# The last expert's six held weight loads are issued in order, and the running sum is loaded from GpSimd's queue and used behind the branch

## The chip, the cores and the metric

The kernel runs on one core of one Trainium2 chip. The metric is device time in microseconds of one launch; the time before is the median of three runs. A profile is one further execution, taken by the hardware profiler. Times inside it are counted from the span's start. The engines are named as in the profile: PE (TensorE matmuls), PEld (its weight loads), DVE (VectorE), ACT (ScalarE), POOL (GpSimd), SP (SyncE, which here only issues transfers).

## The reference, cut to what matters

One layer of a decoder: a token mixer, a layer norm, a mixture of 32 experts of which each token takes four, and a second layer norm. The change touches only the end of the mixture.

```python
def moe_ffn(x2, w_router, b_router, w_gu, b_gu, w_down, b_down):
    ...                                     # top 4 of 32 experts per token, softmax gates
    def expert_block(args):
        tok, e = args
        xb = x_pad[tok]
        h = xb @ w_gu[e] + b_gu[e]          # 1024 -> 2048
        gate = jnp.minimum(h[:, 0::2], SWIGLU_LIMIT)
        up = jnp.clip(h[:, 1::2], -SWIGLU_LIMIT, SWIGLU_LIMIT)
        act = (up + 1.0) * (gate * jax.nn.sigmoid(SWIGLU_ALPHA * gate))
        return act @ w_down[e] + b_down[e]  # 1024 -> 1024
    ...
    out = jax.ops.segment_sum(y, slot_tok, num_segments=t_tok + 1)[:t_tok]

x = layer_norm(DEEPNORM_ALPHA * x + m, ln2_g[l], ln2_b[l])   # m is moe_ffn's output
```

There are 512 tokens of width 1024, all in float32.

## The kernel before, in words

The experts run one after another. Expert e has twelve weight tiles of 1 MB each: eight gu tiles (k = 0 to 7, rows of `w_gu`) and four dn tiles (rows of `w_down`, two k each). `wload` (L585) hands them out in this order over a ring of 19 buffers and issues each load on SP's queue. SP works through its queue strictly in order, and a load is issued only when the third load before it has landed (`PACE` = 3).

For one expert PE runs 24 units: sixteen gu units (in the last expert k by k, two halves `a` = 0 and 1 for each k), then eight dn units (units j = 16 to 23, k = 0 to 7). A unit is two matmuls in the program, which the trace counts as four. Between the units stand the steps of the activation: `act(e, a)` (L1053 to L1057 on DVE and ACT) makes 256 columns of the activation per half, `act_t(e, a)` transposes them on PE (L1030) and copies them to `at` on ACT (L1140). dn units k = 0 to 3 need `act_t(e, 0)`, those with k = 4 to 7 need `act_t(e, 1)`. Each expert's result is then added to `accd`, the running sum in HBM, by an indirect transfer from POOL's queue (L946, a scatter with add).

The last expert's result doesn't go through `accd`. Instead the running sum comes back on chip as two loads of 1 MB (`load_sum`, tiles FT in ring buffers named `gw`), which have to wait for expert 30's scatter. For each of the four blocks t of 128 tokens, `split_sum` makes a rounded high part on ACT (L1259) and the remainder on DVE (blocks 0 to 2) or POOL (block 3) (L1262). `last_sum` (L1264) then adds up in PSUM, per block and half q: gates times the down bias (L1270, from `b`, which needs `b_down`), and the two parts of the sum (L1272). `last_bias` (L1249) makes `b` out of the three small `b_down` loads (L1216): one cast on ACT (L1251) and one subtraction on POOL (L1252). After the last dn unit ACT and DVE make `ys` from the dn result, `last_y` adds it for each block (L1289), and the second layer norm and the stores follow.

Behind unit j = 17 stands a branch on all engines (`tc.If(cmax > 192)`, L1411) to a general path for experts with more than 192 tokens. It isn't taken with these inputs, but every engine has to pass it.

Of the last expert `wload` only allocates the last six tiles (`HELD` = 6: gu k = 6 and 7, and the four dn tiles) and keeps their loads back. `last_loads` (L1209), which runs behind unit 0 of the last expert, issues on SP first the two loads of the sum, then the three of `b_down`, then the six that were held. The splitting of the sum stands behind unit 11 (`BJ`), the sums of block 0 behind unit 15 (`SJ`), those of block 1 behind the branch, those of block 2 behind unit 19. The program's order is the order on each engine: there is no reordering.

Of the kernel before, what the change touches and what calls it, by code (L numbers as in the profile page):

```python
# [33 lines left out]
def hybrid_kernel(ctx, tc, x, w_in, b_in, conv_a, w_out_a, w_pool, scale_pool, conv_c, conv_c_b,  # L34
                  ln_c_g, ln_c_b, w_out_c, b_out_c, w_o, ln1_g, ln1_b, w_router, b_router,
                  w_gu, b_gu, w_down, b_down, ln2_g, ln2_b, out, dbg=None):
    nc = tc.nc
# [451 lines left out]
    for i, (kind, c, post) in enumerate(steps):  # L489
# [7 lines left out]
        if kind == "yb" and (c | 1) not in PLH:  # L497
            while fg:
                q, f, f2 = fg.popleft()
# [28 lines left out]
        while fg:  # L528
            q, f, f2 = fg.popleft()
# [42 lines left out]
    wjobs = []  # L572
# [6 lines left out]
    wn = [0]  # L579
    wpools = [(wB1, "wb1")] * 4 + [(wA, "w")] * 3 + [(wB2, "wb2")] * 2 + [(wA, "w")] + [(wB2, "wb2")] * 2  # L580
    RING = 12 + NB3 + 4

    lds, held = [], []

    def wload(n):  # L585
        for _ in range(n):
            if wn[0] >= len(wjobs):
                return
            key, src = wjobs[wn[0]]
            pool, tag = wpools[wn[0] % RING]  # L590
            shp = [128, 2 * D] if key[0] == "gu" else [128, 2, D]
            t_ = pool.tile(shp, F32, name="w", tag=tag)
            def ld(t_=t_, src=src):
                i = nc.sync.dma_start(t_, src).ins
                if len(lds) >= PACE:
                    tc.add_manual_dep(i, lds[-PACE].name, mybir.DependencyInfo(
                        mybir.DependencyClass.Sync, mybir.DependencyReason.DATA), reason="a few loads under way at a time")
                lds.append(i)
            held.append(ld) if wn[0] >= len(wjobs) - HELD else ld()
            W[key] = t_  # L600
            wn[0] += 1

# [230 lines left out]
    def split_wo(n):  # L833
        for a in range(2):
            wo_split(n, a, *((split, ("wh", "wl")) if n == 3 else (wB2, None)))
        chunks.pop(("wo", n))

    wload(4)
    split_wo(1)
    load_next()  # L840
# [49 lines left out]
    t = NT - 1  # L890
# [311 lines left out]
    def ring(shape, dt, name):  # L1202
        pool, tag = wpools[nring[0] % RING]
        nring[0] += 1
        return pool.tile(shape, dt, name=name, tag=tag)

    FT, FS, GW, FP, LT = [], [], [], [[None, None] for _ in range(NT)], {}

    def last_loads():  # L1209

        GW.extend(ring([128, 2 * D], F32, "gw") for _ in range(3))
        FS.extend(ring([128, 2, D], F32R, "fs") for _ in range(4))
        FT.extend(GW[q].rearrange("p (t d) -> p t d", t=2) for q in range(2))
        load_sum(nc.sync)
        for q in range(3):
            nc.sync.dma_start(GW[2][32 * q:32 * q + 32, 0:D], b_down[0])  # L1216
        for ld in held:
            ld()

    def load_sum(eng):  # L1220
        for q in range(2):
            eng.dma_start(FT[q], accd[256 * q:256 * q + 256, :].rearrange("(t p) d -> p t d", p=128))
# [26 lines left out]
    def last_bias():  # L1249
        raw, b3 = GW[2][:, 0:D], LT["b3"]  # L1250
        nc.scalar.activation(b3[0:96, :], raw[0:96, :], AF.Copy)  # L1251
        nc.gpsimd.tensor_sub(b3[64:96, :], raw[64:96, :], b3[64:96, :].bitcast(F32))  # L1252

    def split_sum(t, h_eng, l_eng):

        f = FT[t // 2][:, t % 2, :]
        h_, l_ = LT["f", t] = [v[:, t % 2, :] for v in FS[t // 2 * 2:t // 2 * 2 + 2]]
        if h_eng is nc.scalar:
            nc.scalar.activation(h_, f, AF.Copy)  # L1259
        else:  # L1260
            h_eng.tensor_copy(h_, f)
        l_eng.tensor_sub(l_, f, h_.bitcast(F32))  # L1262

    def last_sum(t, q, tag, bufs=2):  # L1264

        if FP[t][q] is None:
            FP[t][q] = pse.tile([128, 512], F32, name="fp", tag=tag, bufs=bufs)
        p_ = FP[t][q]
        d = slice(512 * q, 512 * q + 512)
        nc.tensor.matmul(p_, LT["gt"][0:96, t, :], LT["b3"][0:96, d], start=True, stop=False)  # L1270
        for v in LT["f", t]:
            nc.tensor.matmul(p_, identr, v[:, d], start=False, stop=False)  # L1272

    def split_sums():
        for t in range(NT):
            split_sum(t, nc.scalar, nc.gpsimd if t == LSP else nc.vector)

    def sums(t, again=False):
        for q in range(2):
            if again:  # L1280

                nc.tensor.matmul(FP[t][q], LT["gt"][0:96, t, :], LT["b3"][0:96, 0:512], start=False, stop=True)
            last_sum(t, q, *(("gu", 4) if t < 2 else ("tr", 2)))

    def last_y(t):
# [59 lines left out]
    for e in range(E):  # L1345
# [3 lines left out]
        for j in range(NU):  # L1349
# [51 lines left out]
            if last:  # L1401
                if j == 8:
                    last_gates()
                if j == BJ:
                    last_bias()
                    split_sums()
                if j == SJ:
                    sums(0)
                if j == 17:
                    act_t(e, 1)  # L1410
                    with tc.If(cmax > 192, label="rest"):  # L1411
                        general()
                        load_sum(nc.scalar)
                        split_sums()
                        sums(0, again=True)
                    nc.scalar.activation(wrm2, wrm2, AF.Sqrt)
                    sums(1)
                if j == 19:
                    sums(2)
                if j == 21:  # L1420
                    last_sum(3, 0, "dn", 2)
# [84 lines left out]
NB3 = 3  # L1506
LEAD = 3
PACE = 3
HELD = 6
SJ = 15  # L1510
BJ = 11
BC = 3
TQ = 18
# [30 lines left out]
```

## Time and profile before

| | us |
|---|---|
| median of 3 runs | 1798.96 |
| lowest and highest of them | 1793.8, 1801.75 |
| the profiled execution, its own time | 1802.16 |
| its span, first to last instruction | 1800.4 |
| PE busy | 1635.7 (91% of the span) |
| DVE, ACT, POOL busy | 673.1, 326.0, 330.5 |
| mean granted clock of TensorE | 0.962 |

The busy shares are averages over the whole kernel. Everything that the change touches lies in the last 90 us: expert 31 begins at about 1726 us. So the views to read are those of this stretch: a table of short windows, the timelines of single engines (start, length, line, operation, how often; in brackets the idle time before it and what ended it), and what the transfer queues moved.

### The profile page before, as it was taken

The numbers are of one execution on the slowest core, as the hardware profiler recorded it, in microseconds if no ns is written. First come the engines' busy times: TensorE is split into PE (matmuls) and PEld (weight loads), VectorE is DVE, ScalarE is ACT, GpSimd is POOL, SyncE is SP. The second block draws the span as 40 slices with busy tenths as digits, with TensorE's granted clock in tenths as the row PEclk, the third lists the DMA queues.
The fourth block names the chain that finished last, engine by engine and source line by source line (L and its number), as shares of the span: only waits on it lengthen the run. The fifth ranks groups of instructions, "written<-read, shape, count | busy, mean of one in ns | idle before, by whom it ended". The sixth has DMA issues, their size and how long they took to land. (4 is left out here: it accounts for less than half of the span.)

```text
span 1800.4 us, 23991 instructions
## 1 busy us (share of the span) xinstructions
PE 1635.7 (91%) x8967; PEld 853.2 (47%) x8967; DVE 673.1 (37%) x1450; ACT 326.0 (18%) x530; POOL 330.5 (18%) x268
## 2 busy tenths in 40 slices
PE   9999999999998699899998987999899999998973
PEld 7888888777887233333332322333333333333321
DVE  5999999556357221212121211211111211111124
ACT  3222222354233111111110100111010101111111
POOL 0120110676115111110110111011101111110122
PEclk9999999999999799999998998999999999999987
DMA  7232223223286589999999999869979998898992
GB/s 226 83 99 95 91 89 102 86 70 117 94 294 246 188 324 395 396 382 392 322 384 405 398 385 395 344 210 389 401 277 349 389 343 292 333 405 326 396 375 97
DMA packets 140837, 494.50 MB, mean 275 GB/s; under 512 B 10919, under 2 KB 64311, under 8 KB 107711
## 3 DMA queue, kind: packets, MB, share of 16 engines
q1 hardware_dynamic: 128815, 465.03, 67.1%
q0 software_dynamic: 11472, 25.47, 5.7%
q8 instruction: 162, 2.65, 0.6%
q14 instruction: 100, 0.82, 0.1%
q10 hardware_dynamic: 288, 0.52, 0.1%
HBM read 473.82 MB, written 17.17 MB: 273 GB/s over the span
## 5 line engine op out<-in xcount | busy, mean ns | idle before, releaser
L1079 PE MATMUL gu<-w,xt 128*64 128x512 f32 x2048 | 481.4, 615 | 47.0 <-DMA w<-in_w_gu_dram 29.7
L1053 DVE TENSOR_SCALAR ag<-gu 128x256 f32<-128x256 f32 x86 | 36.4, 424 | 789.7 <-PE gu L1079 662.9
L1079 PEld LDWEIGHTS gu<-w,xt 128*64 128x64 f32 x2048 | 150.1, 141 | 349.0 <-issue 276.5
L1086 PE MATMUL dn<-w,at 128*64 128x512 f32 x1024 | 258.8, 637 | 0.0
L482 PE MATMUL acc<-xh,wl 128*128 128x512 f32 x568 | 222.3, 391 | 8.2 <-DVE wl L456 4.0
L480 PE MATMUL acc<-xh,wh 128*128 128x512 f32 x568 | 221.9, 391 | 0.6 <-ACT wh L454 0.6
L481 PE MATMUL acc<-xl,wh 128*128 128x512 f32 x568 | 221.2, 389 | 0.0
L235 DVE SCALAR_TENSOR_TENSOR cc<-v,prm,cc 128x512 f32<-128x512 f32 x240 | 168.1, 762 | 0.0
L1079 PE MATMUL gu<-w,xg 128*32 128x512 f32 (+1 forms) x1024 | 155.5, 594 | 4.0 <-ACT xg L1105 4.0
L456 DVE TENSOR_TENSOR wl<-w,wh 128x1024 fp32r<-128x1024 f32 (+2 forms) x85 | 115.2, 1356 | 89.4 <-ACT wh L454 89.3
L1054 ACT ACTIVATE as<-ag 128x256 f32<-128x256 f32 x86 | 35.6, 414 | 503.6 <-DVE ag L1053 503.6
L1086 PEld LDWEIGHTS dn<-w,at 128*64 128x64 f32 x1024 | 74.2, 144 | 104.2 <-issue 101.7
L482 PEld LDWEIGHTS acc<-xh,wl 128*128 128x128 f32 x568 | 106.6, 188 | 34.6 <-DVE wl L456 7.4
L480 PEld LDWEIGHTS acc<-xh,wh 128*128 128x128 f32 x568 | 106.7, 188 | 23.4 <-ACT wh L454 1.5
L481 PEld LDWEIGHTS acc<-xl,wh 128*128 128x128 f32 x568 | 106.7, 188 | 22.4 <-issue 0.2
L454 ACT ACTIVATE wh<-w 128x1024 fp32r<-128x1024 f32 (+2 forms) x97 | 95.8, 990 | 102.6 <-PE acc L481 92.8
L942 POOL DMA_INDIRECT xg<-x1d,ixw x32 | 31.1, 971 | 371.1 <-DVE ev L983 274.5
L1079 PEld LDWEIGHTS gu<-w,xg 128*32 128x32 f32 (+1 forms) x1024 | 46.8, 120 | 101.0 <-issue 91.7
L1086 PE MATMUL dp<-w,pa 128*32 128x256 f32 (+1 forms) x832 | 79.1, 430 | 9.1 <-ACT pa L1116 9.1
L946 POOL DMA_INDIRECT accd<-y,ix x31 | 47.2, 1523 | 209.1 <-ACTq L1012 105.5
L1030 PE MATMUL tr<-ident,aa 128*128 128x128 f32 x128 | 28.0, 302 | 44.3 <-DVEq L1017 16.7
L1030 PEld LDWEIGHTS tr<-ident,aa 128*128 128x128 f32 x128 | 13.1, 143 | 101.1 <-issue 74.8
(301 smaller groups left out, 1565.3 us busy)
## 6 DMA issues: line engine op xcount, KB each, us to landing
w<-in_w_gu_dram SPq DMA_DIRECT2D x256, 1024.0 KB, 8.4
w<-in_w_down_dram SPq DMA_DIRECT2D x128, 1024.0 KB, 8.7
w<-in_w_in_dram SPq DMA_DIRECT2D x35, 1024.0 KB, 5.0
w<-in_w_out_a_dram SPq DMA_DIRECT2D x4, 1024.0 KB, 5.1
w<-in_w_out_c_dram SPq DMA_DIRECT2D x4, 1024.0 KB, 6.6
w<-in_w_o_dram SPq DMA_DIRECT2D x4, 1024.0 KB, 5.1
xk<-in_x_dram SPq DMA_DIRECT2D x4, 512.0 KB
tk<-in_x_dram SPq DMA_DIRECT2D x4, 512.0 KB, 5.3
```

The lines of the kernel that those rows point to most:

```text
L235: nc.vector.scalar_tensor_tensor(acc, v[:, k:k + T], w, acc, op0=OP.mult, op1=OP.add)
L454: nc.scalar.activation(h_[:, p], src[:, p], AF.Copy)
L456: eng.tensor_sub(l_[:, p], src[:, p], h_[:, p].bitcast(F32))
L480: nc.tensor.matmul(ps, h_[:, j, :], rh[k], start=j == 0, stop=False)
L481: nc.tensor.matmul(ps, h_[:, j, :], rl[k], start=False, stop=False)
L482: nc.tensor.matmul(ps, l_[:, j, :], rh[k], start=False, stop=j == n - 1)
L946: nc.gpsimd.indirect_dma_start(out=rows, out_offset=bass.IndirectOffsetOnAxis(ap=ix, axis=0), in_=src, in_offset=None, compute_op=OP.add)
L1030: nc.tensor.transpose(p_[:, j, :], src(j), ident)
L1053: nc.vector.tensor_scalar(g, hv[:, :, 0], LIMIT, None, op0=OP.min)
L1054: nc.scalar.activation(s, g, AF.Sigmoid, scale=SWA)
L1079: nc.tensor.matmul(self.part(hp, i), x, self.gw(k)[:, c:c + 512], start=start, stop=stop)
L1086: nc.tensor.matmul(self.part(dp, q), x, self.dw(k)[:, self.w * q:self.w * q + self.w], start=k == 0, stop=k == KT - 1)
```

## The change

The six held loads are issued where they stand in the order, on SP behind the others of expert 31. The loads of the sum are issued from POOL's queue in place of SP's; the `b_down` loads stay on SP. The splitting of the sum stands behind the branch, once instead of once before it and once in the general path, and the sums of blocks 0, 1 and 2 stand behind units 18, 19 and 20.

```diff
-    lds, held = [], []
+    lds = []
...
-            held.append(ld) if wn[0] >= len(wjobs) - HELD else ld()
+            ld()
...
         FT.extend(GW[q].rearrange("p (t d) -> p t d", t=2) for q in range(2))
-        load_sum(nc.sync)
         for q in range(3):
             nc.sync.dma_start(GW[2][32 * q:32 * q + 32, 0:D], b_down[0])
-        for ld in held:
-            ld()
+        load_sum(nc.gpsimd)
...
-    def sums(t, again=False):
+    def sums(t):
         for q in range(2):
-            if again:
-
-                nc.tensor.matmul(FP[t][q], LT["gt"][0:96, t, :], LT["b3"][0:96, 0:512], start=False, stop=True)
             last_sum(t, q, *(("gu", 4) if t < 2 else ("tr", 2)))
...
                 if j == BJ:
                     last_bias()
-                    split_sums()
-                if j == SJ:
-                    sums(0)
                 if j == 17:
                     act_t(e, 1)
                     with tc.If(cmax > 192, label="rest"):
                         general()
                         load_sum(nc.scalar)
-                        split_sums()
-                        sums(0, again=True)
+                    split_sums()
                     nc.scalar.activation(wrm2, wrm2, AF.Sqrt)
+                if j == 18:
+                    sums(0)
+                if j == 19:
                     sums(1)
-                if j == 19:
+                if j == 20:
                     sums(2)
                 if j == 21:
                     last_sum(3, 0, "dn", 2)
...
-HELD = 6
-SJ = 15
```

Three places show how the instructions move. First SP's queue at the last expert, before; `w` are weight tiles, `gw<-accd` the loads of the sum, `gw<-in_b_down_dram` those of `b_down`:

```order
L594 DMA w<-in_w_gu_dram 128x2048 x3
L1426 TENSOR_LOAD cmx
L1426 ISA x2
L1222 DMA gw<-accd 128x2x1024 x2
L1216 DMA gw<-in_b_down_dram 32x1024 x3
L594 DMA w<-in_w_gu_dram 128x2048 x2
L594 DMA w<-in_w_down_dram 128x2x1024 x4
L1411 COMPARE_AND_BRANCH
```

And SP's queue at the same place in the changed kernel:

```order
L1012 UNCONDITIONAL_BRANCH
L594 DMA w<-in_w_gu_dram 128x2048 x5
L594 DMA w<-in_w_down_dram 128x2x1024 x4
L1420 TENSOR_LOAD cmx
L1420 ISA x2
L1215 DMA gw<-in_b_down_dram 32x1024 x3
L1403 COMPARE_AND_BRANCH
```

The loads of the sum have left this queue (on POOL they stand directly in front of the subtraction for `b`), and the `b_down` loads, which stood ahead of the six held weights, now stand behind all weights. Second ACT from the last expert's gates to the table load behind the branch, before; `b<-gw` is the cast that needs `b_down`, `fs<-gw` the high parts of the sum, `as` the sigmoid, `at` the copy of the transposes:

```order
L1241 ACTIVATE b_23522<-gT 96x512
L1247 ACTIVATE b_23522<-sT 128x512
L1251 ACTIVATE b_23522<-gw 96x1024
L1259 ACTIVATE fs<-gw 128x1024 x4
L1054 ACTIVATE as<-ag 128x256
L1140 ACTIVATE at<-tr 128x256
L1054 ACTIVATE as<-ag 128x256
L1140 ACTIVATE at<-tr 128x256
L1411 COMPARE_AND_BRANCH
```

The same in the changed kernel, up to the branch:

```order
L1239 ACTIVATE b_23522<-gT 96x512
L1245 ACTIVATE b_23522<-sT 128x512
L1249 ACTIVATE b_23522<-gw 96x1024
L1054 ACTIVATE as<-ag 128x256
L1140 ACTIVATE at<-tr 128x256
L1054 ACTIVATE as<-ag 128x256
L1140 ACTIVATE at<-tr 128x256
L1403 COMPARE_AND_BRANCH
```

The cast from `b_down` keeps its place ahead of both sigmoids; the four high parts have gone from here and stand behind the branch. Third PE behind the branch, before; `fp<-b` is gates times bias, `fp<-fs` the two parts of the sum:

```order
L1411 UNCONDITIONAL_BRANCH x2
L1270 MATMUL fp<-b_23522 128x512
L1272 MATMUL fp<-fs,identr 128x512 x2
L1270 MATMUL fp<-b_23522 128x512
L1272 MATMUL fp<-fs,identr 128x512 x2
L1086 MATMUL dn<-w,at 64x512 x4
L1270 MATMUL fp<-b_23522 128x512
L1272 MATMUL fp<-fs,identr 128x512 x2
```

And in the changed kernel:

```order
L1403 UNCONDITIONAL_BRANCH x2
L1086 MATMUL dn<-w,at 64x512 x2
L1268 MATMUL fp<-b_23522 128x512
L1270 MATMUL fp<-fs,identr 128x512 x2
L1268 MATMUL fp<-b_23522 128x512
L1270 MATMUL fp<-fs,identr 128x512 x2
L1086 MATMUL dn<-w,at 64x512 x2
L1268 MATMUL fp<-b_23522 128x512
L1270 MATMUL fp<-fs,identr 128x512 x2
```

Block 0's sums, which ran before the branch, stand behind it now, and one dn unit stands between the sums of two blocks.

## Rows read from the trace of the kernel before

**Rows 1.** PE, timeline: start, length, operation, count [idle before, what ended it]

```profile
1738.03 1.94 PE L1079 MATMUL gu<-w,xt 128*64 128x512 f32 x8 [0.53 <-DMA w<-in_w_gu_dram]
1748.98 5.36 PE L1079 MATMUL gu<-w,xt 128*64 128x512 f32 x16 [9.01 <-DMA w<-in_w_gu_dram]
1757.34 0.44 PE L1030 MATMUL tr<-ident,aa 128*128 128x128 f32 x2 [3.00 <-DVE aa L1057]
...
1759.11 1.94 PE L1086 MATMUL dn<-w,at 128*64 128x512 f32 x8
1760.98 0.44 PE L1030 MATMUL tr<-ident,aa 128*128 128x128 f32 x2
...
1764.06 0.73 PE L1272 MATMUL fp<-fs,identr 128*128 128x512 f32 x2 [1.88 <-ACTq L1411]
...
1765.43 1.94 PE L1086 MATMUL dn<-w,at 128*64 128x512 f32 x8
1767.30 0.50 PE L1270 MATMUL fp<-b 96*128 96x512 f32 x1
...
1768.89 1.94 PE L1086 MATMUL dn<-w,at 128*64 128x512 f32 x8
...
1771.66 1.94 PE L1086 MATMUL dn<-w,at 128*64 128x512 f32 x8
```

**Rows 2.** SP's queue, timeline of its last loads, same columns

```profile
1737.19 0.89 SPq L1222 DMA_DIRECT2D gw<-accd  x2
1738.12 1.59 SPq L1216 DMA_DIRECT2D gw<-in_b_down_dram  x3
1739.76 0.90 SPq L594 DMA_DIRECT2D w<-in_w_gu_dram  x2
```

**Rows 3.** ACT, timeline of the last expert, same columns

```profile
1746.63 1.06 ACT L1251 ACTIVATE b<-gw 96x1024 fp32r<-96x1024 f32 x1 [9.22 <-DMA gw<-in_b_down_dram]
1747.59 3.88 ACT L1259 ACTIVATE fs<-gw 128x1024 fp32r<-128x1024 f32 x4
1756.06 0.42 ACT L1054 ACTIVATE as<-ag 128x256 f32<-128x256 f32 x1 [4.59 <-DVE ag L1053]
...
1761.45 0.38 ACT L1140 ACTIVATE at<-tr 128x256 f32<-128x256 f32 x1 [2.89 <-PE tr L1030]
1764.14 1.28 ACT L1416 ACT_TABLE_LOAD   x1 [2.31 <-ACTq L1411]
```

**Rows 4.** Windows: length, five engines' busy time, TensorE's clock, DMA share, GB/s

```profile
1735.00:1738.00 3.00, 2.50 (x20) 0.78 (x16) 0.00 (x0) 1.08 (x2) 0.00 (x0) 1.00 0.30 116
1740.00:1749.00 9.00, 0.02 (x2) 0.03 (x2) 0.34 (x1) 2.37 (x3) 1.23 (x1) 0.62 1.03 386
1749.00:1752.40 3.40, 3.40 (x8) 0.98 (x10) 3.40 (x3) 2.47 (x3) 1.91 (x2) 0.50 1.00 416
1752.40:1761.00 8.60, 5.60 (x27) 2.17 (x23) 6.26 (x9) 1.10 (x3) 2.15 (x1) 1.00 0.99 405
```

**Rows 5.** Queues, 1735 to 1738 us: packets, MB, share of 16 engines

```profile
q1 hardware_dynamic: 54, 0.34, 27.5%
```

**Rows 6.** Queues, 1738 to 1761.5 us; GB/s in 40 equal slices, SP's queue q1

```profile
GB/s 112 49 418 418 432 404 411 432 432 411 391 216 307 223 446 432 432 404 418 432 418 377 425 411 425 425 425 411 425 425 418 411 411 432 404 439 390 432 265 35
...
q1 hardware_dynamic: 2064, 8.78, 97.2%
```

**Rows 7.** Queues, 1716 to 1726 us: SP's q1 and POOL's q0 together

```profile
DMA packets 762, 4.24 MB, mean 424 GB/s; under 512 B 74, under 2 KB 74, under 8 KB 420
...
q0 software_dynamic: 279, 1.04, 25.7%
```

**Rows 8.** Splitting and activation: line L1262, POOL and DVE timelines

```profile
L1262 DVE TENSOR_TENSOR fs<-gw,fs x3: 1212/2541/3370, 1748.7 to 1752.3; 128x1024 fp32r<-128x1024 f32 x3
...
1747.77 2.35 POOL L1252 TENSOR_TENSOR b<-gw,b 32x1024 fp32r<-32x1024 f32 x1 [19.19 <-ACT b L1251]
...
1756.86 0.43 DVE L1057 TENSOR_TENSOR aa<-aa,as 128x256 f32<-128x256 f32 x1
```

## The prediction

> **What bounds the kernel now.** I read the tail alone, since nothing before 1726 us changes. PE's timeline comes first: after the matmuls on gu tile 5, which end at 1739.97, PE stands for 9.01 us until 1748.98, waiting for a weight transfer [rows 1]. SP's queue says why: it puts out the two loads of the sum at 1737.19, the `b_down` loads at 1738.12 and only then, at 1739.76, gu tiles 6 and 7 [rows 2]. The windows say what the transfer engines did meanwhile: between 1735 and 1738 they were busy for 0.30 of the time, before and after that for all of it [rows 4], so SP had nothing under way while it waited for the scatter of expert 30. PE's stand also brought its granted clock from 1.00 (2.4 GHz) to 0.50 (1.2 GHz); the last gu matmuls ran at 0.50 up to about 1752.4, 3.4 us after PE started again [rows 4], and took 5.36 us for 16 where 8 had taken 1.94 [rows 1].
>
> ACT's timeline is the one that decides. Its cast of `b_down` waits for the transfer and starts at 1746.63, 2.4 us before PE gets its weights [rows 1, 3]; four high parts follow, then the sigmoid of half 0 at 1756.06 [rows 3]. From there the chain is activation, transpose, copy, dn units; a branch, during which ACT does nothing for 2.31 us [rows 3]; sums and dn units up to 1773.60, the end of the last dn matmul [rows 1]. What follows (`ys`, layer norm, stores) isn't touched: I take it as equal, 26.8 us to the span's end. So I compare one moment, the end of the last dn unit.
>
> **The change part by part.**
>
> *Weights in order.* The 9.01 us wait goes. Tile 6 can be issued as soon as tile 3 has landed, and the hole in the transfers between 1735 and 1738 is filled. The rest of the bytes stay the same. SP's queue moved 8.78 MB (six weights 6.29, sum 2.10, `b_down` 0.39) from about 1739.1, where the GB/s row jumps to 418, to about 1760.8, where it falls [rows 6]: 21.7 us, 0.405 MB/us. At 1735 0.34 MB of older weights were left [rows 5]. Without a hole 9.12 MB at that rate end at 1735 + 22.5 = 1757.5, 3.3 us earlier than before.
>
> *`b_down` goes last.* This is the step that turns the sign. In the changed queue the `b_down` loads stand behind all weights, so theirs are the last bytes of the stream. On ACT the cast still stands ahead of both sigmoids, so the whole activation of the last expert now waits for them. From last byte to cast I take 1.4 us: before, sum and `b_down` (2.49 MB from 1739.1 at 0.405) were through at 1745.2, and the cast started at 1746.63 [rows 3, 6]. So the cast starts at 1757.5 + 1.4 = 1758.9, **12.3 us later** than before. Call this moment L. The gu matmuls are done by about 1745 and wait; that gain is lost whole.
>
> *The sum on POOL's queue.* It costs POOL two issues behind the scatter that it waits for anyway. Queued behind them on POOL is only the subtraction for `b`, which needs the cast. The sum shares the engines with the weights, as the loads for the second layer norm did between 1716 and 1726: 1.04 MB of POOL's and the rest SP's, 424 GB/s together [rows 7], no more than SP's queue draws alone in the stretch of [rows 6]. So another queue brings no extra bandwidth, and the sum delays `b_down` by its full 2.10/0.405 = 5.2 us. If it weren't to share, L would be 1753.7; that is the low end.
>
> The Trainium skill has a ceiling for this stream: "DMA: Bandwidth & Descriptors", section "Specifications", gives 435 GB/s for the fabric and about 358 GB/s for HBM per core. By 435 the end would be 1756.0 and the sum below 1.5 us less; by 358 it would be 3.0 us more, 10.3 in all and so slower by over 0.5%. This trace agrees with neither as a mean: 405 here, and 424 over ten us [rows 6, 7], which the 358 would forbid, so I give that case no chance of its own.
>
> *From L to the last dn unit.* The cast frees ACT after 0.96 (1746.63 to 1747.59), the sigmoid takes 0.42 [rows 3], the multiplication on DVE 0.43 [rows 8]. This multiplication now lies beside POOL's subtraction for `b` (2.35 us); the same DVE operation on the sum took 1.21 us at best and 2.54 and 3.37 beside POOL [rows 8], so I double it: +0.45. Transposes 0.44 [rows 1] at full clock; PE has stood since about 1745, so half clock, 0.88. Copy with its handover 0.5 (0.38 itself [rows 3]). PE starts the dn units at L + 3.75. Two units take 1.94 at full clock [rows 1], 3.88 at half; with the clock coming back 3.4 us after PE's start, as before [rows 4], 2.95: L + 6.7. Transposes 0.40 on top (0.44, overlapping), then the copy starts at L + 7.15. From that copy to ACT's next instruction behind the branch there were 2.69 us (1761.45 to 1764.14 [rows 3]): the high part of block 0 starts at L + 9.85 and takes 1.04 (3.88 for four, a pitch of 0.95). DVE makes block 0's remainder in 1.21, POOL being idle then: L + 12.1.
>
> Before, this splitting lay under PE's waits; its cover is gone, and PE waits for it. dn unit 2 and the bias matmuls fill some of the wait, and cost nothing. From then on it's PE's own work, since ACT's pitch of 0.95 and DVE's 1.21 are shorter than PE's step of a unit and a block's sums: rest of block 0's sums 1.05 (1.37 from 1764.06 to 1765.43 less the part that is done [rows 1]), units 3, 4 and 5 at 0.97, sums of blocks 1 and 2 at 1.59 (1767.30 to 1768.89 [rows 1]), half of block 3 at 0.8, units 6 and 7 at 1.94: 9.9 us. The end is L + 22.0.
>
> **How the numbers follow.** Before, from the cast (1746.63) to the last dn unit (1773.60) it was 26.97 us. Now it is 22.0, **5.0 less**, since no gu matmuls, no waiting for them and no sums of block 0 ahead of the dn units lie in it; but it starts 12.3 later. The balance is **+7.3 us**. The profiled execution took 1802.2 us (span 1800.4 and 1.8 around it) and would take 1809.5. It lay 3.2 above the median, which I take as the scatter of runs; on the median of 1798.96 the forecast is 1806.3.
>
> Bounds of the terms: the stream at 424 GB/s instead of 405, -1.0; at 386, the lowest of the busy windows in [rows 4], +1.1. No half clock after PE's stand, -1.45; another 3.4 us of it after the wait for block 0, +1.7. No slower multiplication, -0.45; block 0's remainder at 2.54, +1.3. Alone that makes +4.4 to +11.4. Half a per cent, about what a measurement of this kernel can tell from no change, is 9.0 us.
>
> **The rivals.**
>
> *The sum takes no share of the weights' time.* Then L is 1753.7 and the balance +2.1: 1801.1. For it: POOL's transfers start later than SP's could. Against it: the common 424 GB/s [rows 7]. In a sentence of its own, the Trainium skill ("DMA: Bandwidth & Descriptors", "Issuing engines are not separate DMA queues") says too that transfers of all issuing engines run on the same 16 engines and interleave, which speaks against this rival and against the reason for the move. Chance 0.10.
>
> *The stall simply goes (faster).* If `b_down` lands before tile 7, by 1743 or so, ACT isn't held. Activation and branch then run from about 1744.5, and the last dn tile is the last thing that PE waits for: bytes through at 1757.5 less the 1.0 us of `b_down`, 1.4 to land, 1.94 for units 6 and 7: 1759.8, or 13.8 less than before, 1785.2. For it: the 9.01 us are the largest wait in the tail. Against it: the change's own order, on SP and on ACT alike. It would need transfers to overtake those that stand ahead. Chance 0.06.
>
> *TensorE stays at 1.2 GHz to the end of the sums (slower).* In the new tail PE works in pieces between waits on ACT and DVE. If the clock isn't raised again before the last dn unit, the two first units take 0.9 more, the second transposes 0.4, the remaining 9.9 us double: +11.2 on the forecast, 1817.5. It decides at PE's first piece after L: if the clock is still at 0.50 when block 0's sums start. For it: 0.50 for 3.4 us of unbroken work [rows 4]. Against it: in 1752.4 to 1761, with 3.00 us of waiting in it, the clock stayed at 1.00 [rows 1, 4]. Chance 0.14.
>
> My own case has 0.70. About 0.50 of it lies within 9.0 us, 0.19 above, 0.01 below. With the rivals: faster 0.07, same 0.60 (the no-share case with it), slower 0.33. The range has to hold 8 in 10: from the no-share case less the scatter of medians, 1799, to the forecast's upper bound with a little of the slow-clock case, 1812.
>
> **What would show it.** In the changed profile no matmul on gu waits 9 us, and the transfers have no hole near 1736. ACT's cast of `b_down` waits some 20 us and starts near 1759, and POOL and both sigmoids come behind it. PE idles from about 1745 to 1761 with the clock falling to 0.50. After the branch PE waits 2 to 4 us for the first `fs`. I am wrong if the cast starts before 1752, if a sigmoid runs before the cast, or if the last dn unit ends before 1775.

## The result and the profile after

The changed kernel takes 1815.45 us (median of 8 runs, 1812.23 to 1819.34), the kernel before 1802.58 us (8 runs, among them the three shown above, 1793.8 to 1807.58). The ratio is 1.0067, with a 95% interval of 1.0047 to 1.0086: slower by 12.9 us. The direction was forecast as the balance (+7.3), but as most likely within half a per cent; the time lies above the range, which ended at 1812.

Where expert 31 begins differs from run to run by several us (1720.7 to 1736.5 in the twelve profiles of this study), whatever the kernel. So I compare traces from the start of expert 31 (its first bias matmul on PE, `gu<-bgp`, at 1725.74 before and 1729.63 after). From there to the end of the span it is 74.7 us before and 87.9 after, 13.2 more, close to the 12.9 between the medians.

PE's timeline of the changed kernel, same columns as in [rows 1]:

```profile
1729.63 0.39 PE L1074 MATMUL gu<-bgp,sel 96*64 96x512 bf16 x2
...
1746.84 1.94 PE L1079 MATMUL gu<-w,xt 128*64 128x512 f32 x8 [0.91 <-DMA w<-in_w_gu_dram]
1767.32 0.69 PE L1030 MATMUL tr<-ident,aa 128*128 128x128 f32 x2 [18.54 <-DVE aa L1057]
1768.54 3.68 PE L1086 MATMUL dn<-w,at 128*64 128x512 f32 x8 [0.53 <-ACT at L1140]
...
1776.83 0.80 PE L1270 MATMUL fp<-fs,identr 128*128 128x512 f32 x1 [2.18 <-ACT fs L1257]
1778.09 0.79 PE L1270 MATMUL fp<-fs,identr 128*128 128x512 f32 x1 [0.47 <-DVE fs L1260]
...
1780.10 1.98 PE L1086 MATMUL dn<-w,at 128*64 128x512 f32 x4
...
1788.64 1.94 PE L1086 MATMUL dn<-w,at 128*64 128x512 f32 x8
```

The 9.01 us wait of [rows 1] is gone: gu tile 7 is worked off by 1748.78, 19.2 us after the start of the expert where it was 28.6. In its place PE waits 18.54 us for the activation, and after the branch 2.18 and 0.47 for the parts of the sum. The last dn unit ends at 1790.58.

ACT's timeline says why:

```profile
1763.50 1.06 ACT L1249 ACTIVATE b<-gw 96x1024 fp32r<-96x1024 f32 x1 [22.02 <-SPq L1403]
1764.46 0.40 ACT L1054 ACTIVATE as<-ag 128x256 f32<-128x256 f32 x1
...
1772.88 0.38 ACT L1140 ACTIVATE at<-tr 128x256 f32<-128x256 f32 x1 [4.09 <-PE tr L1030]
1775.72 3.90 ACT L1257 ACTIVATE fs<-gw 128x1024 fp32r<-128x1024 f32 x4 [2.46 <-ACTq L1403]
```

The cast of `b_down`, first row, has ACT idle for 22.02 us before it, and the sigmoid of half 0 stands directly behind it. (The bracket names an instruction of SP's branch; the cast stands ahead of the branch and doesn't depend on it. What ended at that time is the transfer of `b_down`, as the next views show.) SP's queue, and then windows of the same stretch with the columns of [rows 4]:

```profile
1726.72 12.34 SPq L594 DMA_DIRECT2D w<-in_w_gu_dram  x5
1741.57 10.67 SPq L594 DMA_DIRECT2D w<-in_w_down_dram  x4
1753.15 1.35 SPq L1215 DMA_DIRECT2D gw<-in_b_down_dram  x3
```

```profile
1752.00:1754.00 2.00, 0.00 (x0) 0.00 (x0) 0.00 (x0) 0.00 (x0) 0.00 (x0) 0.60 1.02 422
1758.00:1760.00 2.00, 0.00 (x0) 0.00 (x0) 0.00 (x0) 0.00 (x0) 0.00 (x0) 0.50 1.07 395
1760.00:1762.00 2.00, 0.00 (x0) 0.00 (x0) 0.00 (x0) 0.00 (x0) 0.00 (x0) 0.50 0.62 162
1762.00:1764.00 2.00, 0.00 (x0) 0.00 (x0) 0.00 (x0) 0.50 (x1) 0.00 (x0) 0.50 0.08 25
1768.00:1772.00 4.00, 3.47 (x9) 0.77 (x8) 0.81 (x2) 0.69 (x2) 0.00 (x0) 0.50 0.03 6
1774.00:1776.00 2.00, 0.65 (x3) 0.19 (x1) 0.00 (x0) 0.28 (x1) 0.00 (x0) 1.00 0.00 0
1776.00:1778.00 2.00, 0.80 (x1) 0.29 (x1) 1.19 (x2) 2.00 (x3) 0.00 (x0) 0.57 0.02 4
1778.00:1782.00 4.00, 3.91 (x8) 1.46 (x8) 2.31 (x3) 3.10 (x4) 2.25 (x1) 0.50 0.00 0
1782.00:1784.00 2.00, 2.00 (x8) 1.44 (x6) 0.00 (x0) 0.00 (x0) 0.51 (x1) 0.72 0.00 0
```

The `b_down` loads go out last, the stream runs at about 420 GB/s without a hole, thins out from 1760 and ends in 1762 to 1764, where the cast starts. From 1749.2 (the end of DVE's last step for half 0) to 1763.5, for some 14 us, no engine computes. The clock column has two stretches at 0.50 (1.2 GHz): one that PE enters while it waits and that covers the first two dn units, which take 3.68 us in place of 1.94, and a second one from about 1777 to 1783, behind the wait for the first high part.

### The profile page after: what moved, and what is told of

It reads as the page before. It is cut to its first block, busy times and chain, and to the rows that moved or that the text cites. A ratio compares the mean times of both kernels' runs of the same rounds, so it can differ in the third digit from the quotient of the medians.

```text
span 1817.5 us, 23989 instructions
## 1 busy us (share of the span) xinstructions
PE 1641.5 (90%) x8967; PEld 855.7 (47%) x8967; DVE 676.2 (37%) x1450; ACT 326.2 (18%) x530; POOL 330.8 (18%) x270
## 5 line engine op out<-in xcount | busy, mean ns | idle before, releaser
L1079 PE MATMUL gu<-w,xt 128*64 128x512 f32 x2048 | 476.2, 609 | 41.2 <-DMA w<-in_w_gu_dram 23.7
L1086 PE MATMUL dn<-w,at 128*64 128x512 f32 x1024 | 266.2, 652 | 0.8 <-ACT at L1140 0.5
L482 PEld LDWEIGHTS acc<-xh,wl 128*128 128x128 f32 x568 | 106.6, 188 | 34.3 <-DVE wl L456 7.1
```

What stands on the lines that cost most here:

```text
L482: nc.tensor.matmul(ps, l_[:, j, :], rh[k], start=False, stop=j == n - 1)
L1079: nc.tensor.matmul(self.part(hp, i), x, self.gw(k)[:, c:c + 512], start=start, stop=stop)
L1086: nc.tensor.matmul(self.part(dp, q), x, self.dw(k)[:, self.w * q:self.w * q + self.w], start=k == 0, stop=k == KT - 1)
```

## The experiments

Figures in us "from the start of expert 31" are from PE's and ACT's timelines of each profile; medians and ratios are of timed runs, each against the kernel before on the same chip. Against the change's own ratio (1.0047 to 1.0086) only experiments 1 and 5 lie clear; the intervals of 2, 4, 6, 7, 9 and 10 touch or overlap it, so what these show is read from their traces.

**1. b_down early.**

```diff
         for q in range(3):
-            nc.sync.dma_start(GW[2][32 * q:32 * q + 32, 0:D], b_down[0])
+            nc.gpsimd.dma_start(GW[2][32 * q:32 * q + 32, 0:D], b_down[0])
         load_sum(nc.gpsimd)
```

> The changed kernel with one word altered: the three b_down loads go out on POOL's queue ahead of the loads of the sum, in place of SP's queue behind all weights. Theory (the whole difference hangs on ACT's cast of b_down, which waits for the last bytes of the stream): the cast runs at about 1741, right behind the copies of the gates, ACT is free when the gu matmuls end, and PE waits for the dn weights only. The last dn unit then ends some 13 us before that of the kernel before, as worked out in the rival 'the stall simply goes': about 1789 us against 1802.6 for the kernel before and 1815.5 for the change. Rival 1 (the splitting that now stands uncovered behind the branch is what costs): it still stands there, so the time stays at or above the kernel before, 1803 to 1812. Rival 2 (the sum on POOL's queue slows the stream): no gain, 1812 to 1816.

Measured: 1806.26 us, ratio 1.0005 (0.9984 to 1.0025). The cast goes to 16.3 us, and 10.3 of the 13.2 us are back (77.6 from the start of the expert to the end of the span). But the time isn't below that of the kernel before: the 13 us of gain that I had worked out for "the stall simply goes" were not there. ACT's rows, and two of the branch's own (L1403: count, durations in ns, first and last start), say where they went:

```profile
1755.09 0.42 ACT L1054 ACTIVATE as<-ag 128x256 f32<-128x256 f32 x1 [5.29 <-DVE ag L1053]
...
1762.48 0.38 ACT L1140 ACTIVATE at<-tr 128x256 f32<-128x256 f32 x1 [4.89 <-PE tr L1030]
1767.34 3.90 ACT L1257 ACTIVATE fs<-gw 128x1024 fp32r<-128x1024 f32 x4 [4.47 <-SPq L1403]
```

```profile
L1403 SPq EVENT_SEMAPHORE  x9: 17/17/17, 1764.8 to 1767.2; - x9
...
L1403 ACTq EVENT_SEMAPHORE  x2: 17/17/17, 1766.6 to 1766.7; - x2
...
L1403 ACTq COMPARE_BRANCH  x1: 45/45/45, 1762.5 to 1762.5; - x1
```

The activation is no longer held (the sigmoid waits for DVE and so for the gu matmuls). But ACT needs 4.1 us to pass the branch (1762.5 to 1766.6), while weights still stream, where it had needed 2.5 in the kernel before with idle transfer engines, and its first high part starts only at 1767.34, just behind SP's last event at the branch. The cost of the branch, which I took from a moment when the transfer engines were idle, was wrong for an earlier moment. Besides, `b_down` now lies in the way of gu tiles 5 to 7: 309 to 355 GB/s between 1740 and 1748, and the gu matmuls end at 23.0 us instead of 19.2.

**2. The cast behind the branch.**

```diff
-                if j == BJ:
-                    last_bias()
...
                     split_sums()
+                    last_bias()
                     nc.scalar.activation(wrm2, wrm2, AF.Sqrt)
```

> The changed kernel with b_down still last in SP's queue, but its cast on ACT and its subtraction on POOL moved behind the branch and behind the splitting of the sum. Theory (what costs is not that b_down lands late, but that the cast stands ahead of both sigmoids): the activation runs from about 1749 in the trace of the change, the branch and the splitting are done when b_down lands at 1763.5, and cast, subtraction (beside or behind POOL's remainder of block 3) and 10 us of PE's own work are left: last dn unit at about 1779 in place of 1790.6, so 11 to 12 us below the change, about 1804. Rival (the lateness itself or the uncovered splitting costs): within 3 us of the change, 1812 to 1816.

Measured: 1810.34 us, ratio 1.0033 (1.0014 to 1.0051), about 5 below the change and not 11 to 12. The step in front comes as expected (the second copy of the activation is at 26.0 us where the change has 43.3), so the cast's place on ACT does hold the activation. Most of that is lost again behind the branch:

```profile
1748.31 0.38 ACT L1140 ACTIVATE at<-tr 128x256 f32<-128x256 f32 x1 [3.25 <-PE tr L1030]
1757.64 3.90 ACT L1257 ACTIVATE fs<-gw 128x1024 fp32r<-128x1024 f32 x4 [8.95 <-SPq L1401]
1761.45 1.04 ACT L1249 ACTIVATE b<-gw 96x1024 fp32r<-96x1024 f32 x1
```

```profile
L1401 SPq EVENT_SEMAPHORE  x9: 17/17/17, 1753.6 to 1757.8; - x9
...
L1401 ACTq EVENT_SEMAPHORE  x2: 17/17/17, 1753.5 to 1753.6; - x2
...
L1401 ACTq COMPARE_BRANCH  x1: 45/45/45, 1748.3 to 1748.3; - x1
```

ACT passes the branch at 1753.6, 5.2 us after reaching it, and then its first high part waits four more, until SP's events end. The last of these comes at 1757.8, right behind the last bytes of `b_down` on SP's queue (between 1756 and 1757). The rest is lost because cast and subtraction now stand behind the splitting, on ACT behind four high parts and on POOL behind the remainder of block 3 (2.80 us): PE waits for the bias.

```profile
1766.89 0.80 PE L1268 MATMUL fp<-b 96*128 96x512 f32 x1 [16.00 <-POOL b L1250]
```

The last dn unit ends at 57.6 us, where the change has 61.0.

**3. The splitting behind the branch, alone.** The kernel before with this part of the change:

```diff
                 if j == BJ:
                     last_bias()
-                    split_sums()
-                if j == SJ:
-                    sums(0)
...
                         load_sum(nc.scalar)
-                        split_sums()
-                        sums(0, again=True)
+                    split_sums()
                     nc.scalar.activation(wrm2, wrm2, AF.Sqrt)
-                    sums(1)
-                if j == 19:
-                    sums(2)
+                if j == 18:
+                    sums(0)
+                if j == 19:
+                    sums(1)
+                if j == 20:
+                    sums(2)
```

> The kernel before with one part of the change alone: the splitting of the sum behind the branch, and the sums of blocks 0, 1 and 2 behind units 18, 19 and 20. Weights, sum and b_down are loaded as before, from SP. Theory: little. DVE no longer stands in the way of the activation (it began 1.2 us after the gu matmuls ended) and no sums lie ahead of the first dn units, which gives back some 3 us; the wait for block 0's parts behind the branch takes about as much, and up to 2 us more if the clock falls in it: 1801 to 1806 against 1802.6. Rival 1 (this part is the cost): 1809 or more.

Measured: 1805.70 us, ratio 0.9998 (0.9974 to 1.0022): no difference that the runs can tell. In the trace the second copy comes 3.3 us earlier (32.4 against 35.7), and the last dn unit ends 3.6 us later (51.5 against 47.9), since ACT takes from 1758.50 to 1763.31 from this copy to the first high part, while the last weights stream. So this part costs a little in the trace, not 13 us, and rival 1 falls.

**4. The bias subtraction on DVE.**

```diff
     def last_bias():
         raw, b3 = GW[2][:, 0:D], LT["b3"]
         nc.scalar.activation(b3[0:96, :], raw[0:96, :], AF.Copy)
-        nc.gpsimd.tensor_sub(b3[64:96, :], raw[64:96, :], b3[64:96, :].bitcast(F32))
+
+    def last_bias_low():
+        raw, b3 = GW[2][:, 0:D], LT["b3"]
+        nc.vector.tensor_sub(b3[64:96, :], raw[64:96, :], b3[64:96, :].bitcast(F32))
...
                     act(e, 1)
+                    last_bias_low()
```

> The changed kernel with the 32-row subtraction for the down bias on DVE, behind both halves of the activation, in place of POOL right behind the cast. In the change DVE's multiplication of half 0 took 2.37 us, from 1764.89 to 1767.26, beside POOL's subtraction from 1764.65 to 1766.98, where it takes 0.43 without it. Theory (DVE's two-input operation is held up by POOL's): the multiplication takes 0.43 again, PE starts 1.9 us earlier, and the time falls by 1.5 to 2.5 us, to about 1813.5. Rival (something else held DVE, such as the wait for the sigmoid): the multiplication still takes over 2 us and the time stays at 1815.5.

Measured: 1809.42 us, ratio 1.0034 (1.0009 to 1.0059). POOL's subtraction in the change, and DVE's multiplication of half 0 beside it:

```profile
1764.65 2.33 POOL L1250 TENSOR_TENSOR b<-gw,b 32x1024 fp32r<-32x1024 f32 x1 [21.99 <-ACT b L1249]
...
1764.89 2.37 DVE L1057 TENSOR_TENSOR aa<-aa,as 128x256 f32<-128x256 f32 x1 [15.71 <-ACT as L1054]
```

The multiplication in this experiment:

```profile
1759.06 0.43 DVE L1057 TENSOR_TENSOR aa<-aa,as 128x256 f32<-128x256 f32 x1 [15.34 <-ACT as L1054]
```

0.43 again, and from the cast to the end of the last dn unit 25.3 us in place of 27.1: 1.8, as expected. The median is lower by more than that, 6 us; these runs scatter from 1804 to 1821, the intervals of the two ratios overlap, and the trace accounts for no more than 1.8.

**5. Splitting ahead of the branch, b_down early.**

```diff
                 if j == 17:
                     act_t(e, 1)
-                    with tc.If(cmax > 192, label="rest"):
-                        general()
-                        load_sum(nc.scalar)
                     split_sums()
-                    nc.scalar.activation(wrm2, wrm2, AF.Sqrt)
                 if j == 18:
                     sums(0)
                 if j == 19:
                     sums(1)
+                    with tc.If(cmax > 192, label="rest"):
+                        general()
+                        load_sum(nc.scalar)
+                        split_sums()
+                        sums(0, again=True)
+                        sums(1, again=True)
+                    nc.scalar.activation(wrm2, wrm2, AF.Sqrt)
```

> The early b_down of the first experiment, and the splitting of the sum back ahead of the branch (behind the second half's copy on ACT), the sums of blocks 0 and 1 behind units 18 and 19, and the branch only then; the general path makes the splitting and these sums again. Theory (with b_down early, what eats the gain is everything that stands behind the branch: the engines pass it in 4.1 us while weights stream, ACT's splitting waits for SP to pass it, and PE waits for the splitting): from the start of expert 31 to the end of the span 77.6 us become about 70 to 72, 3 to 5 below the kernel before (74.7), 1798 to 1800 in the median. Rival (the gain was never there, since the dn weights land only at about +32 us after the start of expert 31, and the rest follows from that): 76 us or more, 1803 or more.

Measured: 1798.39 us, ratio 0.9970 (0.9954 to 0.9987) against the kernel before: the one version of the study that beats both kernels, the one before by 0.3%, 5 to 6 us. From the start of expert 31 it is 70.5 us. ACT's rows and its passing of the branch (L1410):

```profile
1750.79 0.38 ACT L1140 ACTIVATE at<-tr 128x256 f32<-128x256 f32 x1 [4.64 <-PE tr L1030]
1751.07 3.89 ACT L1257 ACTIVATE fs<-gw 128x1024 fp32r<-128x1024 f32 x4
1755.28 1.28 ACT L1416 ACT_TABLE_LOAD   x1 [0.32 <-ACTq L1410]
```

```profile
L1410 ACTq EVENT_SEMAPHORE  x2: 17/17/17, 1755.1 to 1755.2; - x2
...
L1410 ACTq COMPARE_BRANCH  x1: 45/45/45, 1751.1 to 1751.1; - x1
```

The high parts follow the copy without a gap, and the passing of the branch lies under them: ACT's sequencer makes its compare at 1751.1, while ACT works, and its events follow 0.2 us after the last high part ends (1754.96). What is left idle there is 0.32 us. So the 4.0 us between compare and events don't give the price of the branch: they are as long as the four high parts are.

**6. PE kept busy.** Extra matmuls, whose result isn't used, in the change:

```diff
+                    warm = pse.tile([128, 512], F32, name="warm", tag="tr")
+                    for _ in range(18):
+                        nc.tensor.matmul(warm, ident, W["dn", e, 0][:, 0, 0:512], start=True, stop=True)
                     act_t(e, 0)
...
                 if j == 18:
+                    warm = pse.tile([128, 512], F32, name="warm", tag="tr")
+                    for _ in range(3):
+                        nc.tensor.matmul(warm, ident, W["dn", e, 0][:, 0, 0:512], start=True, stop=True)
                     sums(0)
```

> The change with 18 extra matmuls on PE between the last gu unit and the first transposes, and three more behind unit 18; their result is used nowhere. They fill PE's wait for the cast. Theory (TensorE at 1.2 GHz costs 3 to 4 us of the stretch from the cast to the last dn unit): the clock stays at 1.00, the first two dn units take 1.94 in place of 3.68, and the stretch from the cast to the end of the last dn unit falls from 27.1 to 23 to 24 us; median about 1812. Rival (the clock costs little there, what is slow is waiting): the stretch stays at 26 to 27 us.

Measured: 1814.53 us, ratio 1.0069 (1.0044 to 1.0094), no better than the change. PE's rows:

```profile
1752.34 17.39 PE L1381 MATMUL warm<-w,ident 128*128 128x512 f32 x36 [3.18 <-DMA w<-in_w_down_dram]
1769.56 0.38 PE L1030 MATMUL tr<-ident,aa 128*128 128x128 f32 x2
1770.48 1.94 PE L1086 MATMUL dn<-w,at 128*64 128x512 f32 x8 [0.53 <-ACT at L1140]
```

From the cast to the end of the last dn unit it is 25.5 us, not 23 to 24. Eighteen were too many: they run on to 1769.73, and the transposes, which could have run from about 1767.1, wait for them. The clock term itself shows: the two dn units take 1.94, and from the first to the last dn unit it is 18.3 us in place of 22.0, 3.8 less. Experiment 9 mends the count.

**7. The sum last on SP's queue.**

```diff
-        load_sum(nc.gpsimd)
+        load_sum(nc.sync)
```

> The change with the two loads of the sum on SP's queue behind b_down, in place of POOL's queue. The order of the weights and the splitting stay as in the change. Theory (the sum on POOL's queue takes its share of the stream and so delays b_down by its whole 5.2 us): the cast starts 4 to 5 us earlier, about 29 us after the start of expert 31 in place of 33.9, and the last dn unit ends as much earlier, since the sum isn't needed before the branch: median 1810 to 1812. Rival (the sum costs the weights nothing on another queue): the cast stays at 33 to 34 us, and the time at 1815.

Measured: 1812.40 us, ratio 1.0036 (1.0015 to 1.0057). The cast starts at 31.1 us against 33.9 (33.5 to 34.9 in experiments 4, 6, 9 and 10, which have `b_down` last too). So the sum does take its share of the stream from another queue, but moving it behind `b_down` gives 2.8 us and not 4 to 5. The windows show the stretch in which the `b_down` loads run, with the first part of the sum beside them; it is slow:

```profile
1756.00:1758.00 2.00, 0.00 (x0) 0.00 (x0) 0.00 (x0) 0.00 (x0) 0.00 (x0) 0.50 1.06 338
1758.00:1760.00 2.00, 0.00 (x0) 0.00 (x0) 0.00 (x0) 0.00 (x0) 0.00 (x0) 0.50 1.07 229
1760.00:1762.00 2.00, 0.00 (x0) 0.00 (x0) 0.00 (x0) 0.00 (x0) 0.00 (x0) 0.50 1.00 180
1762.00:1764.00 2.00, 0.00 (x0) 0.00 (x0) 0.00 (x0) 0.80 (x1) 0.00 (x0) 0.50 0.98 346
```

The edit doesn't take the whole sum out of the way either. SP issues it at 1754.50, right behind `b_down` and before that has landed, and of its 2.10 MB SP's queue moved 1.27 after 1763.2, when the cast started. Some 0.8 MB thus still ran beside `b_down`. The 1.27 MB that did get out of the way are worth 3.0 us at 420 GB/s, about what the cast gained.

**8. The general path's reload from POOL's queue.** Experiment 2 with one word altered in the path that isn't taken:

```diff
                         general()
-                        load_sum(nc.scalar)
+                        load_sum(nc.gpsimd)
```

> The second experiment (cast behind the branch) with one word altered: in the general path, which isn't taken, the sum is loaded again from POOL's queue in place of ACT's. In the second experiment ACT had passed the branch at 1753.6, but its first high part started at 1757.64, when SP had passed it too. Theory (on the path around the general part SP sets the semaphores of the loads that ACT would have issued, and SP gets there only when its own last load has landed): with POOL's queue in its place the first high part starts within 1 us of ACT's passing the branch, about 31 to 32 us after the start of expert 31 in place of 35.4. Rival (the high parts waited for the sum itself to land): it stays at 35.

Measured in one execution, 1822.88 us (from the start of expert 31 to the end of the span 84.6 us, the same as in experiment 2): the first high part stays at 35.3 us.

```profile
1771.80 3.90 ACT L1257 ACTIVATE fs<-gw 128x1024 fp32r<-128x1024 f32 x4 [9.14 <-SPq L1401]
```

```profile
L1401 SPq EVENT_SEMAPHORE  x9: 17/17/17, 1767.8 to 1771.9; - x9
...
L1401 ACTq EVENT_SEMAPHORE  x2: 17/17/17, 1767.3 to 1767.4; - x2
```

Again it starts as SP's events end, 4.4 us after ACT has passed. That is the value of the rival, but the rival's reason falls too: POOL issued the two loads of the sum from 1747.96 to 1749.43, and from there to landing they took (the view of their line, L1220)

```profile
DMA to landing us min/median/max: 10.1/12.3/14.4
```

So the sum was there by 1764, nearly 8 us before the high part. My own reason isn't borne out, but not excluded either: the general path also loads weights into these buffers from ACT's queue, and the edit left that. Which of SP's events releases ACT stays open; that the high part starts within 0.2 us of the last of them holds in experiments 1, 2 and 8. In the other profiles with the splitting behind the branch SP's events end before ACT's, and the high part starts within 0.3 us of those.

**9. Subtraction on DVE and PE kept busy.** Experiments 4 and 6 together, with 12 and 2 extra matmuls.

> The change with both: the subtraction for the bias on DVE behind the activation, as in the fourth experiment, and extra matmuls on PE, 12 ahead of the first transposes and 2 behind unit 18, fewer than in the sixth experiment, where the last of them ran 2.4 us beyond the multiplication that PE waits for. Theory (what the forecast had missed in the stretch from the cast to the last dn unit is the multiplication held up beside POOL, 1.8 us, and the clock, 3.8 us from the first dn unit on): this stretch takes 21 to 22.5 us, as forecast (22.0), in place of 27.1; the cast itself stays at 33 to 35 us after the start of expert 31; median about 1810. Rival (the two overlap, or PE waits for something else): 24 us or more.

Measured: 1808.88 us, ratio 1.0027 (1.0005 to 1.0048). ACT's cast and PE's last two dn units:

```profile
1757.07 1.06 ACT L1249 ACTIVATE b<-gw 96x1024 fp32r<-96x1024 f32 x1 [21.70 <-SPq L1410]
...
1777.70 1.94 PE L1086 MATMUL dn<-w,at 128*64 128x512 f32 x8
```

The cast stays at 34.3 us; from it to the end of the last dn unit it is 22.6 us in place of 27.1. That is 0.1 above the upper end that I had written down, and 0.6 above the forecast's 22.0; the two extra matmuls behind unit 18 ran at half clock and held PE until the first sums.

**10. Splitting ahead, b_down late.** Experiment 5 with `b_down` back on SP's queue behind the weights.

```diff
-            nc.gpsimd.dma_start(GW[2][32 * q:32 * q + 32, 0:D], b_down[0])
+            nc.sync.dma_start(GW[2][32 * q:32 * q + 32, 0:D], b_down[0])
```

> The fifth experiment (splitting, and sums of blocks 0 and 1, ahead of the branch) with the b_down loads back on SP's queue behind all weights, as in the change. With the change, the first and the fifth experiment it makes a square: b_down late or early, splitting behind or ahead of the branch. Theory (late b_down holds the whole activation, wherever the splitting stands): the cast stays at 33 to 35 us after the start of expert 31, and from there it's 24 to 25 us to the last dn unit, since the high parts start right behind the second copy: about 85 us from the start of expert 31 to the end of the span, median about 1812, far from the 70.5 of the fifth. Rival (the place of the splitting was the larger part in the fifth): 78 us or less.

Measured: 1809.56 us, ratio 1.0039 (1.0017 to 1.0061), 83.8 us from the start of the expert. The cast is back at 34.2. From it to the end of the last dn unit it is 22.6 us, less than the 24 to 25 expected: PE doesn't wait for the splitting behind a branch any more, and the second stretch at half clock is gone (1.00 from 1768 to 1772).

ACT's passing of the branch, with idle transfer engines:

```profile
L1410 ACTq EVENT_SEMAPHORE  x2: 17/17/17, 1770.6 to 1770.7; - x2
...
L1410 ACTq COMPARE_BRANCH  x1: 45/45/45, 1766.7 to 1766.7; - x1
```

From compare to events it is 3.9 us, as in experiment 5, where weights streamed: in both the events come when the high parts are done. With the change and experiments 1 and 5 there is a square:

| us from the start of expert 31 to the end of the span | splitting behind the branch | ahead of it |
|---|---|---|
| `b_down` behind all weights | 87.9 (the change) | 83.8 (experiment 10) |
| `b_down` early | 77.6 (experiment 1) | 70.5 (experiment 5) |

The kernel before has 74.7. The place of `b_down` is worth 10.3 and 13.3 us, that of the splitting 4.1 and 7.1, more where nothing else holds the chain.

## Why the prediction was right or wrong, point by point

**What decides, right.** The cast of `b_down` waits for the last bytes and holds the activation. The forecast put it 12.3 us later; counted from the start of expert 31 it moved from 20.9 to 33.9, 13.0 later. Experiments 1 and 2 show both halves: with `b_down` early the cast comes early, with the cast out of the way the activation goes ahead.

**The stream, nearly right, by luck: errors that cancel.** The weights and the sum run faster than the 0.405 MB/us I took (about 420 GB/s), and `b_down` runs slower, so that its end thins out (162 and 25 GB/s above): the last 0.36 MB take 3 us, from 1760 to 1763. I had counted `b_down` as 0.39 MB like any other bytes, 1.0 us; that it runs slower stood in [rows 6], where the stream falls to between 216 and 307 GB/s around 1745, just before the cast. And from the last bytes to the cast it is about 0.5 us, not the 1.4 that I had worked out with these loads at full rate. The Trainium skill's ceiling of 435 GB/s ("DMA: Bandwidth & Descriptors", "Specifications") lies about as far above the main part of the stream as my 405 lay below it, and says nothing of its end.

**From the cast to the last dn unit, wrong: 27.1 us, not 22.0.** This is the step that failed. The path was the one forecast; two of the terms on it were too small.
- The multiplication beside POOL's subtraction. I doubled 0.43; it took 2.37, until POOL was through (1764.65 and 2.33, so 1766.98). It isn't slowed in proportion but held for what is left of POOL's instruction: 1.5 us more than forecast. Experiment 4 takes it away and gains 1.8. The trace before had it already: of the three remainders in [rows 8] the first, from 1748.66, took 2.54 and ended 1.1 us after POOL's subtraction did (1750.12), about the 1.21 that it takes alone.
- The clock. I had one stretch of half clock, and put a second one behind the wait for block 0 among the bounds only (+1.7). Both came. The first covered the two dn units in full (3.68, not 2.95), 0.7 more than forecast. The second is the larger miss: from PE's taking up the remainder of block 0 (1778.09) to the end of the last dn unit it was 12.5 us, where I had added up 9.9 at full clock. Experiment 6 keeps the clock at 1.00 over the first dn units and shortens the way from the first to the last one by 3.8 us, of which the forecast had about 1.

With both mended, experiment 9 takes 22.6 us, so these two terms hold nearly all of the miss. (The sum up to the first dn unit has a slip besides: its terms make 3.64, not 3.75.) The rival of 1.2 GHz to the end of the sums was half right: the clock fell twice, but came back in between.

**The branch.** The forecast had 2.69 us from the copy to the next instruction on ACT and 2.84 were measured, in a moment without transfers.

**The rivals.** The sum's share: it does take one (experiment 7), so that rival falls. The 2.8 us there don't speak against my 5.2 for the whole of it, since only 1.27 of the 2.10 MB got out of the way. The faster rival had the wrong price, not only a small chance: even where `b_down` lands early, experiment 1 gains nothing on the kernel before. I had worked it out by the last weights alone and left out the branch under a running stream and the uncovered splitting behind it. Experiment 5, which moves the splitting ahead as well, ends at 43.3 us where the rival had about 34.

**The time.** The range was counted from 1798.96, the median of three runs; over eight it is 1802.58. Of the 9.1 us between 1806.3 and 1815.45, 3.6 are that, and nearly all the rest is the step above. Counted from 1802.58 the range would have ended at 1815.6, just above the measured time, with the step no less wrong.

## What to carry to other kernels

When transfers are reordered on a queue, look at what becomes last and who consumes it: a small load that stood early by accident may feed an instruction at the head of an in-order engine, and everything behind it then waits for the last byte of the stream, whatever it needs itself. Work that is moved behind a branch loses more than its cover: it waits until the engines have passed, and that takes longest while transfers run. When adding up PE's work after a long wait, count its first steps at 1.2 GHz, and reckon with a second such stretch behind a further wait: here one came behind a wait of 2.2 us, though in the kernel before the clock stayed at 1.00 over a wait of 3.0 us [rows 1, 4].

## What the runs showed of the hardware

- Passing a branch that isn't taken took ACT 2.4 to 2.8 us, from its compare to its events behind it, where the transfer engines were idle (before, 1761.5 to 1764.0; after, 1772.9 to 1775.5; experiments 4, 6, 7 and 9), and 4.1 to 5.2 us where weights streamed for most of that time (experiments 1, 2 and 8: 4.1, 5.2, 5.0; in experiment 3, where the stream ended in the middle, 4.5). What makes the difference is open; no run here isolates it.
- DVE's multiplication of two tiles in SBUF stood for the whole remainder of a POOL subtraction, 2.37 us for 0.43, though the latter works on 32 partitions (the same 2.37 or 2.38 in experiments 6, 7 and 10). The Trainium skill ("GPSIMD Engine Reference", "Specifications") says that POOL shares its SBUF interfaces with VectorE and contends with instructions that have two SBUF inputs; the trace agrees, and experiment 4 gives the size.
- While three loads of 32 partitions by 4 KB, 0.39 MB in all, ran in it, the stream fell from about 420 to between 180 and 338 GB/s for some 6 us (experiment 7), with the transfer engines busy all the time; at the end of the changed kernel's stream the last 0.36 MB took 3 us. Why they are so slow wasn't tried.
